# A list scheduler's table of durations is set to other figures

## The chip, the cores and the metric

The kernel runs on one core of one Trainium2 chip. The metric is the device time of one execution in microseconds; the time of a kernel is the median of its runs.

## The reference

One sample of 1024 latent tokens with 1024 channels goes through two layers, in fp32. A prefix of 256 context tokens goes through the first layer's mixer as well. Each layer is a token mixer and then a gated FFN with a convolution, and each of these sub-layers is normalized, modulated by a conditioning vector and added back with a gate.

```python
# layer 0: bidirectional gated linear recurrence (RG-LRU)
ul = seq_conv(hl @ w_x, conv_w, conv_b, CONV_A_PAD)        # latent tokens
uc = seq_conv(hc @ w_x, conv_w, conv_b, CONV_A_PAD)        # context tokens
r = sigmoid(u @ w_r + b_r); i = sigmoid(u @ w_i + b_i)     # blocks of 256 channels, each direction
log_a = 8 * r * log_sigmoid(lam); a = exp(log_a)
h_t = a * h_prev + sqrt(-expm1(2 * log_a)) * (i * u)       # forward and reverse, context first
y = (gelu(hl @ w_gate) * (h_fwd + h_bwd)) @ w_out
# layer 1: short gated convolution
y = (g_b * conv3(g_c * v)) @ w_out
# both layers
y = (silu(conv(g)) * v) @ w_down                           # g, v = h @ w_up, 2816 channels each
```

A modulation is `h * (1 + scale) + shift`; shift, scale and gate are columns of `silu(c) @ ada_w + ada_b`.

## The kernel before

Channels lie on the 128 partitions and tokens along the free axis, so the stream `x` is eight tiles of 128 x 1024. Every fp32 product is three fp32r matmuls over a rounded part and a remainder of both operands (hi·hi, lo·hi, hi·lo). ScalarE writes the rounded part (`wh` of weights, `bh`, `uh`, `hch` of tokens) and VectorE the remainder (`wl`, `bl`, `ul`, `hcl`). The FFN's products are cut into blocks of which seven products replace eight; `s` are its temporaries and its staged weights.

The first layer's mixer goes by the string `ORDER`: `g0` to `g7` are gate products, `x` the products of `w_x` for latent tokens, `ctx` the modulation of the context tokens and their products (`ctx_apply`, L701), `r0` to `r7` the recurrence of 128 channels each (`ri`, L770). `start` (L565) does the norm and the first products; its last part, `shifts`, ends in `softplus` (L522), a row of tiny VectorE operations on 128 x 16 (`sp`) that makes the recurrence's columns. `conv_a` (L710) evicts a product on ScalarE and adds three taps on VectorE (`u<-banks`, `u<-acct`, `u<-uc`; `uc` for context tokens). `ri` evicts into tiles `mx` on ScalarE, multiplies and scans (`TENSOR_TENSOR_SCAN`) on VectorE and puts `x<-x,mx` at its end. A conditioning column is a `dot` on VectorE: a row of weights times `c`, summed (`raw,modc<-raw,ccb`, `acct,mod<-acct,cb`).

All these calls only record operations in a `Plan` (L50 to L178), so that every instruction has line 163. `record` finds what each operation must follow, and ties every matmul to the one before it. `flush` (three times: before the tiles of the recurrence, before the FFN, and at the end) puts them in order. It gives each operation a duration from `cost`, and between engines a delay from `lag`. An operation's `due` time is counted back from the matmuls, which follow each other at their cost. Then, step by step, it takes the engine whose best operation would end first, and issues on it, of those that can start before that end, the one with the earliest `due`:

```python
e = min(best, key=best.get)
i = min((i for i in queue[e] if times(e, i)[0] < best[e]), key=lambda i: (due[i], i))
self.done[i] = free[e] = times(e, i)[1]
```

The engines then run their lists in that order, each waiting for the semaphores that its operations need. The figures of `cost` and `lag` set the order alone; no instruction waits for a modelled time.

Of the kernel before, what the change touches and what calls it, by code (L numbers as in the profile page):

```python
# [8 lines left out]
F32 = mybir.dt.float32  # L9
# [40 lines left out]
class Plan:  # L50
# [48 lines left out]
    @staticmethod  # L99
    def cost(engine, op, a, k):  # L100

        if engine == "sync":
            return 4 * int(np.prod(a[0].shape)) / 360e3
        n = max(int(np.prod(v.shape[1:])) for v in list(a) + list(k.values()) if isinstance(v, bass.AP))
        if engine == "tensor":
            n = a[2].shape[-1]
            return max(n, 128) / 2400 * (4 if a[2].dtype == F32 else 1)
        if engine == "scalar":
            return 0.09 + n * 0.85e-3 + (0.09 if "accum_out" in k else 0)
        if engine == "gpsimd":  # L110
            return 0.15 + n * (2.1e-3 if op == "tensor_tensor" else 0.84e-3)
        return 0.07 + n * (6.25e-3 if op == "reciprocal" else 1.05e-3)

    @staticmethod
    def lag(a, b):

        return 0.0 if a == b else 0.95 if a == "sync" else 1.9 if b == "sync" else 0.2

    def flush(self):
        ops, first, last = self.ops, self.todo, len(self.ops)  # L120
# [1316 lines left out]
```

## Time and profile before

| | us |
|---|---|
| median of 3 runs | 2076.04 |
| lowest and highest run | 2074.9, 2076.44 |
| the profiled execution | 2077.46 |
| its span | 2075.7 |
| TensorE busy | 2035.4 (98%) |
| VectorE busy | 1763.0 (85%) |
| ScalarE busy | 1050.3 (51%) |

The span reaches from the first instruction to the last one of the profiled execution; its time has 1.8 us more around it. TensorE's granted clock is 0.993 of full speed over the span. The busy shares are means over stretches of different kind: the mixer of the first layer takes the first 396 us, the FFNs with the second mixer nearly all of the rest.

### The profile page before, as it was taken

The page shows a single profiled execution, that of the slowest core. Times are in us where ns is not written, and L with a number is a line of the kernel's source. Part 1 is how long each engine was busy: PE and PEld are TensorE (multiplying, and loading weights), DVE is VectorE, ACT ScalarE, POOL GpSimd, SP SyncE. Part 2 cuts the span into 40 slices and gives each one's busy share as a digit, 9 for nine tenths or more (in the row PEclk, how much of TensorE's full clock was granted, in tenths as well). Part 3 has the DMA queues.
Part 4 walks back from the last instruction along what each step waited for, and adds up shares of the span by engine and source line. Part 5 has one row for each costly group of instructions (what it writes and reads, how often), then busy time and mean ns, then how long its engine had stood idle before and what let it go on. Part 6 is the DMA issues. An engine that isn't in the chain of part 4 may idle for free.

```text
span 2075.7 us, 25028 instructions
## 1 busy us (share of the span) xinstructions
PE 2035.4 (98%) x9218; PEld 1682.5 (81%) x9218; DVE 1763.0 (85%) x2624; ACT 1050.3 (51%) x1574; POOL 0.2 (0%) x4
## 2 busy tenths in 40 slices
PE   9899988999999999999999999999999999999998
PEld 7688877787888888878888788888888888878888
DVE  7998999889888898798679988868988887688867
ACT  6456878546544444535255433435544444464345
POOL 0000000000000000000000000000000000000000
PEclk9999999999999999999999999999999999999999
DMA  7464222641344554655361346652233433474345
GB/s 299 155 211 151 72 84 92 208 143 55 119 142 149 170 178 163 181 184 173 92 197 57 122 163 201 224 189 77 88 131 126 143 136 113 136 233 144 111 141 164
DMA packets 103418, 307.05 MB, mean 148 GB/s; under 512 B 10368, under 2 KB 14720, under 8 KB 103168
## 3 DMA queue, kind: packets, MB, share of 16 engines
q1 hardware_dynamic: 103296, 305.46, 44.5%
q8 instruction: 72, 1.18, 0.2%
q14 instruction: 50, 0.41, 0.1%
HBM read 248.80 MB, written 56.62 MB: 147 GB/s over the span
## 4 chain that ended last, share of the span: by engine, by line
PE 82%; DVE 10%; ACT 4%; issue 2%; DMA 1%; SPq 0%; DVEq 0%; ACTq 0%
PE banks L163 82%; DVE mx L163 2%; ACT mx L163 2%; DVE x L163 2%; DVE u L163 1%; DVE wl L163 1%; DVE bl L163 1%; DVE raw L163 1%; DMA s<-bd 1%; ACT bh L163 1%; ACT L163 0%; DVE ul L163 0%; DVE cs L163 0%; DVE acct L163 0%; DMA x<-in_xs 0%
## 5 line engine op out<-in xcount | busy, mean ns | idle before, releaser
L163 PE MATMUL banks<-bl,wh 128*128 128x512 f32 (+1 forms) x2720 | 1050.4, 386 | 6.8 <-DVE bl L163 6.8
L163 PE MATMUL banks<-bh,wh 128*128 128x512 f32 (+1 forms) x2720 | 1053.0, 387 | 3.1 <-ACT wh L163 1.7
L163 PE MATMUL banks<-bh,wl 128*128 128x512 f32 (+1 forms) x2720 | 1050.0, 386 | 1.9 <-DVE wl L163 1.8
L163 PEld LDWEIGHTS banks<-bl,wh 128*128 128x128 f32 x2720 | 511.0, 188 | 117.7 <-DVE bl L163 14.7
L163 PEld LDWEIGHTS banks<-bh,wh 128*128 128x128 f32 x2720 | 511.1, 188 | 108.1 <-ACT wh L163 2.1
L163 PEld LDWEIGHTS banks<-bh,wl 128*128 128x128 f32 x2720 | 511.0, 188 | 108.0 <-DVE wl L163 6.8
L163 ACT ACTIVATE wh<-raw 128x512 fp32r<-128x512 f32 (+2 forms) x386 | 275.6, 717 | 476.3 <-PE banks L163 384.2
L163 DVE TENSOR_TENSOR wl<-raw,wh 128x512 fp32r<-128x512 f32 (+2 forms) x386 | 303.4, 795 | 60.7 <-ACT wh L163 57.3
L163 DVE SCALAR_TENSOR_TENSOR x<-banks,mod,x 128x512 f32<-128x512 f32 (+1 forms) x184 | 132.6, 726 | 90.4 <-PE banks L163 89.6
L163 ACT ACTIVATE s<-banks 128x512 f32<-128x512 f32 x174 | 103.7, 596 | 194.7 <-PE banks L163 191.3
L163 ACT ACTIVATE wh<-s 128x512 fp32r<-128x512 f32 x216 | 135.6, 628 | 110.5 <-DVE s L163 63.6
L163 DVE TENSOR_TENSOR wl<-s,wh 128x512 fp32r<-128x512 f32 x216 | 148.6, 689 | 37.7 <-ACT wh L163 34.1
L163 DVE TENSOR_TENSOR s<-s,banks 128x512 f32<-128x512 f32 x158 | 107.9, 684 | 37.2 <-PE banks L163 36.9
L163 DVE SCALAR_TENSOR_TENSOR x<-s,vec,x 128x504 f32<-128x504 f32 x132 | 96.4, 741 | 10.2 <-ACT x L163 9.0
L163 DVE SCALAR_TENSOR_TENSOR acct<-acct,cb 128x1024 f32<-128x1024 f32 x69 | 84.1, 1219 | 4.4 <-DMA acct<-in_ada 4.4
L163 PE MATMUL banks<-uh,wh 128*128 128x512 f32 (+1 forms) x192 | 70.8, 369 | 8.3 <-ACT mx L163 7.1
L163 PE MATMUL banks<-ul,wh 128*128 128x512 f32 (+1 forms) x192 | 70.4, 367 | 3.1 <-DVE ul L163 3.1
L163 PE MATMUL banks<-uh,wl 128*128 128x512 f32 (+1 forms) x192 | 70.2, 366 | 0.0
L163 ACT ACTIVATE bh<-s 128x512 fp32r<-128x512 f32 x88 | 51.5, 624 | 34.3 <-DMA s<-bd 32.9
L163 ACT ACTIVATE bh<-x,cols 128x512 fp32r<-128x512 f32 x64 | 45.1, 722 | 37.2 <-DVE cols L163 22.1
L163 DVE TENSOR_TENSOR x<-x,s 128x512 f32<-128x512 f32 x90 | 61.0, 686 | 0.8
L163 DVE TENSOR_TENSOR bl<-s,bh 128x512 fp32r<-128x512 f32 x88 | 57.2, 685 | 4.2 <-ACT bh L163 4.1
(152 smaller groups left out, 1708.0 us busy)
## 6 DMA issues: line engine op xcount, KB each, us to landing
raw<-in_wup SPq DMA_DIRECT2D x92, 512.0 KB, 3.5
acct<-in_ada SPq DMA_DIRECT2D x69, 512.0 KB, 3.5
bd<-x SPq DMA_DIRECT2D x48, 512.0 KB, 3.2
s<-bd SPq DMA_DIRECT2D x44, 512.0 KB, 4.4
raw<-in_wdn SPq DMA_DIRECT2D x32, 512.0 KB, 4.2
raw<-in_wdn SPq DMA_DIRECT2D x40, 384.0 KB, 3.4
raw<-in_wbi SPq DMA_DIRECT2D x26, 512.0 KB, 3.9
xd<-x SPq DMA_DIRECT2D x48, 256.0 KB, 2.5
```

The costliest lines, as they stand in the source:

```text
L163: getattr(getattr(self.tc.nc, e), op)(*a, **k)
```

## The change

Only `cost` and `lag` change. A fp32r matmul of n columns is put at (n + 32)/2400 us in place of max(n, 128)/2400. A ScalarE operation costs 0.84 ns a column in place of 0.85, no longer 0.09 us more where it sums, and 0.1 us more for each bias or scale that is a column of its own. On VectorE a scan costs 2.07 ns a column, other operations but the reciprocal 1.04 in place of 1.05, and 0.06 us more for each scalar that is a column. What follows a load on another engine may start 2.0 us after it in place of 0.95. The rows for GpSimd, which has no operation in the plan, are gone.

```diff
--- before.py
+++ after.py
@@ -104,17 +104,17 @@
         n = max(int(np.prod(v.shape[1:])) for v in list(a) + list(k.values()) if isinstance(v, bass.AP))
         if engine == "tensor":
             n = a[2].shape[-1]
-            return max(n, 128) / 2400 * (4 if a[2].dtype == F32 else 1)
+            return max(n, 128) / 2400 * 4 if a[2].dtype == F32 else (n + 32) / 2400
         if engine == "scalar":
-            return 0.09 + n * 0.85e-3 + (0.09 if "accum_out" in k else 0)
-        if engine == "gpsimd":
-            return 0.15 + n * (2.1e-3 if op == "tensor_tensor" else 0.84e-3)
-        return 0.07 + n * (6.25e-3 if op == "reciprocal" else 1.05e-3)
+            columns = sum(0.1 for name in ("bias", "scale") if isinstance(k.get(name), bass.AP))
+            return 0.09 + n * 0.84e-3 + columns
+        columns = sum(0.06 for name in ("scalar", "scalar1") if isinstance(k.get(name), bass.AP))
+        return 0.07 + n * {"reciprocal": 6.25e-3, "tensor_tensor_scan": 2.07e-3}.get(op, 1.04e-3) + columns
 
     @staticmethod
     def lag(a, b):
 
-        return 0.0 if a == b else 0.95 if a == "sync" else 1.9 if b == "sync" else 0.2
+        return 0.0 if a == b else 2.0 if a == "sync" else 1.9 if b == "sync" else 0.2
 
     def flush(self):
         ops, first, last = self.ops, self.todo, len(self.ops)
```

TensorE's list is the same before and after. The lists of the other engines differ in the order alone. Three places on VectorE follow.

The first place is VectorE around the modulation of the context tokens. `sp` is softplus, `u<-uc` and `u<-acct` are conv taps of the products behind `shifts`, `raw,modc<-raw,ccb` a dot for the context's columns `cols`, and `cs_104`, `hcl` the context tokens before and after the split. Before:

```order
L163 SCALAR_TENSOR_TENSOR u<-acct,vec,u 128x1022
L163 SCALAR_TENSOR_TENSOR u<-uc,vec,u 128x1022
L163 SCALAR_TENSOR_TENSOR raw,modc<-raw,ccb 128x1024 x2
L163 TENSOR_TENSOR cols<-modc,vec 128x8
L163 TENSOR_TENSOR cols<-cols,vec 128x8
L163 SCALAR_TENSOR_TENSOR cs_104<-xc,cols,cs_104 128x256
L163 TENSOR_TENSOR cols<-modc,vec 128x8
L163 SCALAR_TENSOR_TENSOR cs_104<-xc,cols,cs_104 128x256
L163 TENSOR_TENSOR wl<-raw,wh 128x1024
L163 SCALAR_TENSOR_TENSOR cs_104<-xc,cols,cs_104 128x256 x2
L163 SCALAR_TENSOR_TENSOR hcl<-cs_104,cols,hch 128x256 x2
```

and in the change, where two taps, a `wl`, two dots and ten operations of softplus stand just ahead of this piece:

```order
L163 TENSOR_SCALAR sp<-sp 128x16
L163 TENSOR_TENSOR sp<-sp 128x16
L163 TENSOR_SCALAR sp<-vec 128x16
L163 SCALAR_TENSOR_TENSOR sp<-sp 128x16
L163 SCALAR_TENSOR_TENSOR u<-acct,vec,u 128x1023
L163 SCALAR_TENSOR_TENSOR u<-uc,vec,u 128x1023
L163 SCALAR_TENSOR_TENSOR raw,modc<-raw,ccb 128x1024 x2
L163 TENSOR_TENSOR cols<-modc,vec 128x8
L163 TENSOR_TENSOR cols<-cols,vec 128x8
L163 SCALAR_TENSOR_TENSOR cs_104<-xc,cols,cs_104 128x256
L163 TENSOR_TENSOR cols<-modc,vec 128x8
L163 SCALAR_TENSOR_TENSOR cs_104<-xc,cols,cs_104 128x256 x2
```

The rest of softplus, two more taps and a `wl` have moved ahead of the last dots, and so of `cols`, `cs_104` and `hcl`.

The second place is VectorE between the recurrences of two channel tiles (`uc` and `u` are the two inputs of a recurrence, `mx` its tiles). Before:

```order
L163 SCALAR_TENSOR_TENSOR mx<-mx,uc 128x256
L163 SCALAR_TENSOR_TENSOR mx<-mx,u 128x1024
L163 TENSOR_TENSOR mx<-mx 128x1024
L163 TENSOR_TENSOR x<-x,mx 128x1024
L163 SCALAR_TENSOR_TENSOR acct,mod<-acct,cb 128x1024
L163 SCALAR_TENSOR_TENSOR mx<-mx,u 128x1024
```

and now:

```order
L163 SCALAR_TENSOR_TENSOR mx<-mx,uc 128x256
L163 SCALAR_TENSOR_TENSOR acct,mod<-acct,cb 128x1024
L163 SCALAR_TENSOR_TENSOR mx<-mx,u 128x1024
L163 TENSOR_TENSOR mx<-mx 128x1024
L163 TENSOR_TENSOR x<-x,mx 128x1024
L163 SCALAR_TENSOR_TENSOR mx<-mx,u 128x1024
```

The dot `acct,mod<-acct,cb`, which stood behind `x<-x,mx`, has moved ahead of the scan of `u` whose result goes into that `x`. A few rows further down come the `u<-banks` taps of a `w_x` product. Before:

```order
L163 SCALAR_TENSOR_TENSOR u<-mx,u 128x1024
L163 TENSOR_TENSOR mx<-mx 128x1280
L163 TENSOR_TENSOR u<-u,mx 128x1024
L163 SCALAR_TENSOR_TENSOR u<-banks,vec,u 128x1023
L163 SCALAR_TENSOR_TENSOR u<-banks,vec,u 128x1022
L163 SCALAR_TENSOR_TENSOR u<-banks,vec,u 128x1023
L163 TENSOR_TENSOR wl<-raw,wh 128x1024
L163 SCALAR_TENSOR_TENSOR uc<-mx,uc 128x256
```

and now:

```order
L163 SCALAR_TENSOR_TENSOR u<-mx,u 128x1024
L163 SCALAR_TENSOR_TENSOR uc<-mx,uc 128x256 x2
L163 SCALAR_TENSOR_TENSOR u<-banks,vec,u 128x1023
L163 SCALAR_TENSOR_TENSOR u<-banks,vec,u 128x1022
L163 SCALAR_TENSOR_TENSOR u<-banks,vec,u 128x1023
L163 SCALAR_TENSOR_TENSOR acct,mod<-acct,cb 128x1024
L163 TENSOR_TENSOR mx<-mx 128x1280
L163 TENSOR_TENSOR u<-u,mx 128x1024
```

The taps have moved ahead of `mx<-mx` and `u<-u,mx`, and a `uc<-mx,uc` has come ahead of the taps.

The third place is VectorE at the last two recurrences, where the first operands of the `w_out` product are split (`bl_87`). Before:

```order
L163 TENSOR_TENSOR u<-u,mx 128x1024
L163 TENSOR_TENSOR wl<-raw,wh 128x1024
L163 SCALAR_TENSOR_TENSOR uc<-mx,uc 128x256
L163 TENSOR_TENSOR uc<-uc,mx 128x256
L163 SCALAR_TENSOR_TENSOR mx<-mx,uc 128x256
L163 SCALAR_TENSOR_TENSOR mx<-mx,u 128x1024
L163 TENSOR_TENSOR bl_87<-x,bh_86 128x512
L163 TENSOR_TENSOR wl<-raw,wh 128x1024
L163 TENSOR_TENSOR bl_87<-x,bh_86 128x512 x6
```

and now:

```order
L163 TENSOR_TENSOR bl_87<-x,bh_86 128x512
L163 TENSOR_TENSOR wl<-raw,wh 128x1024
L163 TENSOR_TENSOR bl_87<-x,bh_86 128x512 x2
L163 SCALAR_TENSOR_TENSOR u<-mx,u 128x1024
L163 TENSOR_TENSOR bl_87<-x,bh_86 128x512
L163 TENSOR_TENSOR wl<-raw,wh 128x1024
L163 SCALAR_TENSOR_TENSOR uc<-mx,uc 128x256
L163 TENSOR_TENSOR u<-u,mx 128x1024
L163 TENSOR_TENSOR uc<-uc,mx 128x256
L163 SCALAR_TENSOR_TENSOR mx<-mx,uc 128x256
L163 TENSOR_TENSOR bl_87<-x,bh_86 128x512
L163 SCALAR_TENSOR_TENSOR mx<-mx,u 128x1024
```

Of the `wl<-raw,wh` rows the second of each piece is the same instruction. Five rows of the scan chain stand behind it now, and `bl_87` rows ahead of it.

## Rows read from the trace of the kernel before

**Rows 1.** The busy time of each engine, its share of the span and its instructions
```profile
PE 2035.4 (98%) x9218; PEld 1682.5 (81%) x9218; DVE 1763.0 (85%) x2624; ACT 1050.3 (51%) x1574; POOL 0.2 (0%) x4
```

**Rows 2.** Busy time by stretch (length, then PE, PEld, DVE, ACT, POOL, granted clock, DMA)
```profile
126.00:142.00 16.00, 14.04 (x67) 11.14 (x65) 15.76 (x36) 8.29 (x13) 0.00 (x0) 1.00 0.61 197
142.00:160.00 18.00, 18.00 (x137) 18.00 (x138) 16.69 (x35) 8.17 (x10) 0.00 (x0) 0.91 0.58 178
...
208.00:253.00 45.00, 45.00 (x217) 37.91 (x216) 44.50 (x46) 36.92 (x38) 0.00 (x0) 1.00 0.25 82
...
899.00:2068.00 1169.00, 1166.58 (x5284) 967.02 (x5284) 956.58 (x1455) 539.25 (x873) 0.00 (x0) 1.00 0.44 143
```

**Rows 3.** TensorE's waits, 103 to 396 us: total, times, longest (us)
```profile
PE banks L163 <- ACT mx L163: 7.1, 2, 4.8
PE banks L163 <- DVE ul L163: 3.1, 1, 3.1
...
PE banks L163 <- DVE hcl L163: 1.8, 4, 0.9
```

**Rows 4.** The chain of waits in order of time: start, length, what
```profile
141.96 47.25 PE banks L163 x293
...
1148.00 710.65 PE banks L163 x3135
```

**Rows 5.** Timeline of VectorE, 94 to 103 us: start, length, operation, [idle before <-releaser]
```profile
96.32 2.60 DVE L163 SCALAR_TENSOR_TENSOR u<-banks,vec,u 128x1023 f32<-128x1023 f32 x2 [0.94 <-ACT u L163]
98.83 1.22 DVE L163 SCALAR_TENSOR_TENSOR raw<-raw,ccb 128x1024 f32<-128x1024 f32 x1
```

**Rows 6.** Timeline of VectorE, 142 to 161 us
```profile
143.35 0.17 DVE L163 TENSOR_SCALAR sp<-sp 128x16 f32<-128x16 f32 x1
...
144.50 1.22 DVE L163 TENSOR_TENSOR wl<-raw,wh 128x1024 fp32r<-128x1024 f32 x1
...
150.44 0.17 DVE L163 TENSOR_SCALAR sp<-sp 128x16 f32<-128x16 f32 x1
...
151.87 1.28 DVE L163 SCALAR_TENSOR_TENSOR u<-acct,vec,u 128x1023 f32<-128x1023 f32 x1
...
159.07 1.27 DVE L163 SCALAR_TENSOR_TENSOR u<-uc,vec,u 128x1023 f32<-128x1023 f32 x1
```

**Rows 7.** Timeline of TensorE near 142 and 889 us
```profile
141.96 0.38 PE L163 MATMUL banks<-hcl,wh 128*128 128x256 f32 x1 [0.91 <-DVE hcl L163]
...
889.29 0.50 PE L163 MATMUL banks<-bh,wh 128*128 128x512 f32 x1 [1.67 <-ACT wh L163]
```

**Rows 8.** Timeline of VectorE, 250 to 372 us
```profile
250.78 1.48 DVE L163 TENSOR_TENSOR mx<-mx 128x1280 f32<-128x1280 f32 x1
...
253.31 3.91 DVE L163 SCALAR_TENSOR_TENSOR u<-banks,vec,u 128x1023 f32<-128x1023 f32 x3
...
352.93 1.20 DVE L163 TENSOR_TENSOR u<-u,mx 128x1024 f32<-128x1024 f32 x1
...
356.82 2.35 DVE L163 TENSOR_TENSOR_SCAN mx<-mx,u 128x1024 f32<-128x1024 f32 x1
...
359.91 1.23 DVE L163 TENSOR_TENSOR wl<-raw,wh 128x1024 fp32r<-128x1024 f32 x1 [0.15 <-ACT wh L163]
...
371.85 0.69 DVE L163 TENSOR_TENSOR bl<-x,bh 128x512 fp32r<-128x512 f32 x1 [0.91 <-ACT bh L163]
```

**Rows 9.** Timeline of ScalarE, 243 to 896 us
```profile
243.18 4.16 ACT L163 ACTIVATE mx<-mx,sp 128x1280 f32<-128x1280 f32 x3 [1.06 <-DVE x L163]
...
251.00 1.19 ACT L163 ACTIVATE u<-banks,vec 128x1024 f32<-128x1024 f32 x1
...
358.81 1.06 ACT L163 ACTIVATE wh<-raw 128x1024 fp32r<-128x1024 f32 x1 [2.75 <-PE banks L163]
...
887.57 1.15 ACT L163 ACTIVATE bh<-s 128x512 fp32r<-128x512 f32 x2 [2.68 <-DMA s<-bd]
...
895.56 1.15 ACT L163 ACTIVATE bh<-s 128x512 fp32r<-128x512 f32 x2 [1.30 <-DMA s<-bd]
```

## The prediction

> **What bounds the kernel now.** I read the busy times first, then a table of stretches, then what TensorE waited for, then the chain of waits, and last single places on VectorE, ScalarE and TensorE. The reader should see in the first that TensorE (PE) is busy 98% of the span, so that only 2075.7 − 2035.4 = 40.3 us of it are idle [rows 1]. The diff leaves TensorE's own list of instructions as it is: the planner ties every matmul to the one before. So the time changes only by making those 40 us larger or smaller. The table of stretches shows where the others are the limit [rows 2]. From 126 to 142 us VectorE (DVE) is busy 15.76 of 16 us: it works without a pause on the shift of the normalized stream, the column sums for the conditioning (the `dots`) and the context tokens. From 208 to 253 us it is busy 44.50 of 45. From 899 to 2068 us TensorE has only 2.4 us of idle in 1169. The FFN is therefore TensorE's, and the first 400 us belong to VectorE nearly as much. TensorE's waits between 103 and 396 us confirm it: 7.1 us on ScalarE's (ACT) `mx`, 3.1 on VectorE's `ul`, 1.8 in four waits on VectorE's `hcl` [rows 3]. The chain shows what a delay there is worth. Behind the last `hcl` wait stand 47.25 us of TensorE work without a gap, and the FFN has 710.65 us in one piece [rows 4]. So lateness at 142 us cannot be made up until 189 us, and what is late at 396 us stays late to the end.
>
> **The change part by part.** No instruction is added or taken out; 1417 of 2512 VectorE instructions, 465 of 1544 on ScalarE and 178 of 648 loads and stores stand elsewhere in their engine's list, most by one or two places. I walked the new lists with the durations of the trace. Places where nothing late results I cost at nothing; their cover is TensorE's list, which is contiguous there.
>
> 1. At 95 us VectorE waits 0.94 us for ScalarE before three conv steps [rows 5]. Two dots move ahead of these steps and fill the wait. A dot takes 1.22 us, so VectorE gains the wait once, and the first conv step is late by 2 x 1.22 − 0.94 = 1.5 us, with slack behind it. Worth between 0 and −0.94; I take −0.5.
>
> 2. From 127 to 160 us lies the main cost. Before, VectorE does two conv steps, four context dots and then at once the chain `cols`, `cs`, `hcl` of the context tokens, for which TensorE waits. The 14 remaining tiny softplus steps come later, in two groups, 144.50 − 143.35 = 1.15 us and 151.87 − 150.44 = 1.43 us long, and two more conv steps later still, 1.28 and 1.27 us [rows 6]. Now all of these stand ahead of the last context dots. That is 1.15 + 1.43 + 1.28 + 1.27 = 5.1 us more VectorE work before the first `hcl`, on an engine with no idle time to take it. TensorE already waits for `hcl`, the last time 0.91 us [rows 7], so its lateness passes on whole: **+5.1**. It then goes into the 47.25 us piece [rows 4]; the work that left 143 to 160 us gives nothing back, because TensorE has 18.00 of 18 us there [rows 2]. Lower bound: only softplus counts, if the conv steps find idle time, 2.6. Upper bound: TensorE's granted clock, 0.91 in 142 to 160 us [rows 2], falls as much once more behind the longer wait, 18 x 0.09 = 1.6, so 6.7. I take 5.1, as both rows show VectorE full.
>
> 3. At 243 us a dot (1.22 us as in [rows 5]) moves ahead of the scan that ends in `x<-x,mx`; ScalarE's three `mx` activations already wait 1.06 us for that `x` [rows 9]. They come that much later. Behind them ScalarE now evicts the conv bank (`u<-banks`) before the second of two square roots, about as long as a dot, so it delivers `u` at the same 251.00 + 1.19 = 252.2 us as before. But VectorE comes to its conv steps 2.1 us sooner: two multiplies, 253.31 − 250.78 = 2.53 us, went behind them [rows 8], and a step on 256 columns, which I put at 0.4 us, came ahead. It waits for `u` from 251.2 to 252.2: **+1.0** of idle on a saturated engine. Lower bound 0, if idle time further on absorbs it; upper 1.2, the dot.
>
> 4. At 359 us `wl<-raw,wh` needs ScalarE's `wh`, which itself waits 2.75 us for TensorE, and VectorE waits only 0.15 us for it [rows 8, 9]. In the new list less VectorE work stands ahead of that `wl`. Five steps of the scan chain went behind it, the first at 352.93 us and the last to 359.17 us, 6.24 us less one other `wl` of 1.22, so 5.0 us; four `bl` of 0.69 us came ahead, 2.8 [rows 8]. VectorE stands until `wh` comes, 5.0 − 2.8 = 2.2 us. It gets back the 0.91 us that it waited at 371.85 us [rows 8]: **+1.3**, since the scan chain behind decides when the mixer ends. Bounds 0 (TensorE frees `wh` sooner) and 2.2.
>
> 5. In the FFN's second part, at 889.29 us, TensorE waits 1.67 us for a `wh` [rows 7]. That `wh` now stands ahead of two `bh` which wait 2.68 us for a load, so the wait goes [rows 9]. But two other `bh` slip behind a pair that starts only at 895.56 us after its own load [rows 9], some 3 us later than they ran, and by the slack of TensorE there I expect a new wait of about 2 us. Net **+0.3**, bounds −1.7 and +1.7. Everywhere else in the FFN the moved pieces are a few tenths long and run ahead of use.
>
> Sum: −0.5 + 5.1 + 1.0 + 1.3 + 0.3 = +7.2 us. The profiled execution took 2077.46 us, so it would take 2084.7; it lies 1.4 above the median of the runs, 2076.04, which becomes **2083.2 us**. Lower ends together: −0.94 + 2.6 + 0 + 0 − 1.7 = 0, 2076.0; upper ends: 0 + 6.7 + 1.2 + 2.2 + 1.7 = 11.8, 2087.8.
>
> **The rivals.** *No change.* All that moves is covered: TensorE's 98% is the same list, and whatever idle time VectorE has between 160 and 396 us takes up what is late. For it: [rows 1], and the long pieces in [rows 4]. Against it: the wait on `hcl` is a wait of TensorE itself, and nothing before 189 us can absorb it. It would leave the 5.1 us at 142 us, give back most of it before 396 us, and end within 2076 to 2080.
>
> *Faster.* The new table prices scans at twice the old figure and column operands separately, so that the VectorE and ScalarE steps of the scans may come in an order which is right where the old one was not. The place is 253 to 352 us: TensorE waits there 7.1 us on `mx` and 3.1 on `ul` [rows 3]. If those waits vanish, −10.2, and the push of part 2 stays, +4.6 with part 1, the time is 2076.0 − 5.6 = 2070.4. It decides from the point at which more than 4.6 of the 10.2 us go. For it: ul's matmuls come from work which the new list puts about 1 us earlier. Against it: the chain into these waits goes through VectorE, which is full before them, and its work to be done by then is the same. More than the 40 us of idle can't be had: in the piece of 710.65 us 3135 matmuls follow each other every 710.65 / 3135 = 0.227 us with nothing to wait for [rows 4], and no order of the other engines shortens that. The Trainium skill (Perfetto Trace Analysis, Identifying the Most-Contended Engine) holds the busy share of matmuls a poor measure of the room left on TensorE and points, among others, to the busy share of weight loads. By that share, 81% here [rows 1], some 19% of 2076, 394 us, would be room for a better order; the long piece says that it is not, and the rule gets no chance of its own.
>
> *Slower still.* The FFN's seams miss their loads: part 5 comes to its upper end, 1.4 us more than I take, and parts 2 and 4 as well, 1.6 and 0.9 more. It gives 2083.2 + 3.9 = 2087.1 and is inside the range.
>
> **How the numbers follow.** About 0.2% (4.15 us) is what a measurement of this kernel tells from no change, so `same` is 2071.9 to 2080.2. My forecast with its upper cases has 0.60; it needs part 2 whole and no more than half of it given back. No change has 0.27: the walk through the lists is long, and each slack in it was read from one execution. Faster has 0.13: a walk with fixed durations shows new waits more readily than vanished ones. The range leaves out the outer half of the faster case and a little above the upper ends: 2072 to 2088.5. The slower case's own range is 2080.2 to 2088.5.
>
> **What would show it.** Right: in the changed kernel TensorE waits about 5 us in all for the first `hcl` near 140 to 147 us, and its long piece starts near 147 us instead of 142. VectorE waits about 1 us for ScalarE's `u` near 258 us, and over 2 us for a `wh` near 365 us; the long piece of TensorE work that opens the FFN starts some 7 us late, and the FFN is as long as before. Wrong: the long piece starts at 142 to 143 us, in which case part 2 had slack that I didn't see; or it starts late, and TensorE's waits on `mx` and `ul` shrink by as much; or the FFN itself changes by over 2 us.

## The result, and the profile after

The changed kernel takes 2086.73 us (median of 4 runs, 2084.51 to 2088.53), the kernel before 2075.89 (4 runs, 2074.9 to 2076.44). The ratio is 1.0051 with an interval of 1.0039 to 1.0063: 10.6 us slower, between 8.1 and 13.1. Run once more (e11 below) it gave 1.0049 (1.0036 to 1.0061). The forecast was +7.2 us: the direction is right, the size lies just under the interval.

The page of the changed kernel's profile (an execution of 2084.51 us, the shortest of its four) answers to [rows 1]:

```profile
span 2082.7 us, 25041 instructions
...
PE 2037.4 (98%) x9218; PEld 1685.3 (81%) x9218; DVE 1765.1 (85%) x2624; ACT 1055.5 (51%) x1574; POOL 0.2 (0%) x4
```

The same matmuls, and 45.3 us without one where there were 40.3. The busy shares would let nobody find the loss. The chain of waits does, beside [rows 4] (start, length, what):

```profile
148.04 46.14 PE banks L163 x290
...
403.15 63.38 PE banks L163 x282
...
1153.90 699.94 PE banks L163 x3088
```

The long piece that began at 141.96 us begins at 148.04, but three matmuls further on in the list; the same matmul is 5.6 us late. The FFN's first piece, at 396.14 us before, begins at 403.15, 7.0 late, and its longest, at 1148.00 before, 5.9 late. So in these two executions the loss is made before 400 us and the FFN adds nothing to it. Nor is it one lateness kept. TensorE's matmuls come in the same order in both kernels, so they can be compared one by one: the changed kernel's are 5.0 us late at 189 us, 3.7 at 260 and 7.0 at 396 (times of the kernel before). A part of what the first 150 us lose is taken up, and the recurrences lose 3.3 us anew behind 260 us. Of TensorE's waits from 103 to 406 us (total, times, longest) [rows 3] are the counterpart:

```profile
PE banks L163 <- ACT mx L163: 10.8, 2, 6.2
PE banks L163 <- DVE ul L163: 3.6, 3, 2.1
PE banks L163 <- DVE u L163: 3.0, 1, 3.0
PE banks L163 <- DVE bl L163: 2.5, 1, 2.5
PE banks L163 <- DVE hcl L163: 2.0, 2, 1.8
```

The first `hcl` in VectorE's timeline of the kernel before (start, length, operation, idle before and its releaser):

```profile
136.33 0.87 DVE L163 SCALAR_TENSOR_TENSOR hcl<-cs,cols,hch 128x256 fp32r<-128x256 f32 x2
```

and in the changed kernel the places that steps 1 to 4 of the prediction name:

```profile
95.24 0.62 DVE L163 SCALAR_TENSOR_TENSOR cs<-u,cols,cs 128x384 f32<-128x384 f32 x1 [1.20 <-DMA u<-in_w]
...
130.31 0.17 DVE L163 TENSOR_SCALAR sp<-sp 128x16 f32<-128x16 f32 x1
...
134.01 1.28 DVE L163 SCALAR_TENSOR_TENSOR u<-acct,vec,u 128x1023 f32<-128x1023 f32 x1
135.20 1.28 DVE L163 SCALAR_TENSOR_TENSOR u<-uc,vec,u 128x1023 f32<-128x1023 f32 x1
...
142.01 0.87 DVE L163 SCALAR_TENSOR_TENSOR hcl<-cs,cols,hch 128x256 fp32r<-128x256 f32 x2
...
256.98 3.92 DVE L163 SCALAR_TENSOR_TENSOR u<-banks,vec,u 128x1023 f32<-128x1023 f32 x3 [0.89 <-ACT u L163]
...
365.03 1.22 DVE L163 TENSOR_TENSOR wl<-raw,wh 128x1024 fp32r<-128x1024 f32 x1 [1.70 <-ACT wh L163]
```

The last steps of softplus and two taps stand between 130.31 and 136.4 us, and the first `hcl` comes after them, at 142.01 instead of 136.33 us, 5.7 late. The waits forecast at 1.0 us for `u` and 2.2 us for a `wh` are there with 0.89 and 1.70 us. TensorE, at the first place and at the seam in the FFN:

```profile
142.54 0.39 PE L163 MATMUL banks<-hcl,wh 128*128 128x256 f32 x1 [1.79 <-DVE hcl L163]
...
901.77 0.50 PE L163 MATMUL banks<-bh,wh 128*128 128x512 f32 x1 [1.49 <-ACT bh L163]
```

The wait for `hcl` is only 1.79 us although `hcl` is 5.7 late. TensorE had become late before: its granted clock was at the lower level, 0.50, from 103 to 107 us (length, then busy time of PE, PEld, DVE, ACT, POOL, granted clock, DMA), in the changed kernel

```profile
103.00:107.00 4.00, 3.94 (x12) 3.43 (x13) 3.90 (x6) 2.88 (x7) 0.00 (x0) 0.50 0.48 151
```

and at full speed in the kernel before:

```profile
103.00:107.00 4.00, 4.00 (x21) 3.31 (x21) 3.90 (x8) 3.57 (x7) 0.00 (x0) 1.00 0.81 243
```

Those 4 us had 12 matmuls instead of 21, and that cost nothing that can be seen, since `hcl` came later still: in the second profile of the changed kernel (e11) the granted clock of the same 4 us was 0.76, and the long piece begins at 148.00 us all the same. There TensorE waits 1.15 us for a `wl` near 129 us, as it does not in the first profile, and again 1.79 for the first `hcl`. At the seam, the wait of 1.67 us at 889.29 us [rows 7] is gone and one of 1.49 us has come for the `bh` that slipped, as step 5 had it.

### The profile page after: what moved, and what is told of

It reads as the page before. It is cut to its first block, busy times and chain, and to the rows that moved or that the text cites. A ratio compares the mean times of both kernels' runs of the same rounds, so it can differ in the third digit from the quotient of the medians.

```text
span 2082.7 us, 25041 instructions
## 1 busy us (share of the span) xinstructions
PE 2037.4 (98%) x9218; PEld 1685.3 (81%) x9218; DVE 1765.1 (85%) x2624; ACT 1055.5 (51%) x1574; POOL 0.2 (0%) x4
## 4 chain that ended last, share of the span: by engine, by line
PE 79%; DVE 15%; ACT 3%; issue 2%; DMA 1%; SPq 0%; DVEq 0%; ACTq 0%
PE banks L163 79%; DVE mx L163 3%; DVE x L163 3%; DVE u L163 2%; DVE bl L163 2%; DVE wl L163 2%; ACT mx L163 1%; DVE acct L163 1%; DVE raw L163 1%; DVE ul L163 1%; DVE s L163 1%; DMA s<-bd 1%; ACT L163 0%; DVE cs L163 0%; DMA x<-in_xs 0%
## 5 line engine op out<-in xcount | busy, mean ns | idle before, releaser
L163 PE MATMUL banks<-uh,wh 128*128 128x512 f32 (+1 forms) x192 | 69.6, 362 | 10.8 <-ACT mx L163 10.8
L163 DVE TENSOR_TENSOR x<-x 128x512 f32<-128x512 f32 x88 | 60.4, 687 | 1.1
```

The lines of the kernel that those rows point to most:

```text
L163: getattr(getattr(self.tc.nc, e), op)(*a, **k)
```

## The experiments

`flush` runs three times: up to about 170 us (norm, shifts, context), to about 400 us (recurrences), and from the first FFN on. The experiments work out the orders of both tables in full, each with its own clocks, and issue one of them in each of the three parts. All zeros gives the order before, all ones that of the change.

```diff
+    PICK = (1, 0, 0)
     def flush(self):
+        plans = [self.plan(t) for t in (0, 1)]
+        out = plans[self.PICK[self.turn]]
+        for i in out:
+            engine, op, a, k = self.ops[i][:4]
+            getattr(getattr(self.tc.nc, engine), op)(*a, **k)
+        self.turn += 1
```

Microseconds below are the ratio less one, times 2076; in brackets its interval.

**One part at a time** (`PICK` is (1, 0, 0), (0, 1, 0), (0, 0, 1)).

> The new table orders only the first part of the program (up to about 170 us: norm, shifts, softplus, context products), the old one the recurrences and the FFNs. Theory A (the softplus steps and two conv taps ahead of the context chain are the main cost): TensorE's long piece starts 4 to 6 us later than in the kernel before, and the time is 4 to 6 us longer. Theory B (what is late there is taken up in the recurrences, and the changed recurrences or FFN make the loss): the long piece is late as well, but the time is within 2 us of the kernel before.

> The new table orders only the recurrences (about 170 to 400 us). Theory A: +1 to +2.5 us (the dot ahead of a scan, and the wait for a wh near 359 us). Theory B (the recurrences make the loss): +5 us or more. A third one, that the new prices of scans and columns help here and are hidden by the late start: -1 to -3 us.

> The new table orders only the part from the first FFN on (about 400 us to the end). Theory A: within 1 us of the kernel before, since the one profile of the changed kernel has its FFN 0.3 us shorter. Theory C (the four runs of the changed kernel scatter over 4 us where those before scatter over 1.5, so the FFN's order makes it late in most executions): +2 to +4 us, with a like scatter.

The first part alone: +5.2 us [+3.1 to +7.3]; TensorE's long piece begins at 147.53 us. The recurrences alone: +3.1 [+1.2 to +5.0]. The FFNs alone: +2.3 [+0.4 to +4.2]. The three make 10.6, the change's own figure; each is known to some 2 us, and within that the parts add. By its time, theory B (within 2 us) falls for the first part. The chain of its profile shows less than its time does:

```profile
147.53 45.36 PE banks L163 x290
...
398.98 85.15 PE banks L163 x378
...
1863.91 204.15 PE banks L163 x1038
```

Matmul for matmul that is 5.1 us late at the long piece (it too begins three matmuls further on), and 2.8 at the start of the FFN and 2.0 behind its last seam, which are at 396.14 and 1861.92 us before. So in this pair of executions nearly half of the first part's lateness is taken up before the FFN, 1.4 us of it by the end of the long piece. There the kernel before loses time of its own: both have a granted clock of 0.76 from 142 to 149 us, but in the kernel before that spell lies behind the last wait for `hcl`, and in e1 ahead of it. The traces also make the gap smaller than it is by the medians: the profile of the kernel before is 1.4 us longer than its median, that of e1 1.1 shorter.

In the second run's profile TensorE is 0.5 us early at 189 us and 3.2 late at 396. Its waits for `mx` are 10.7 us, as in the change, where the first run has the 7.1 of the kernel before. VectorE's timeline of that run shows both waits of steps 3 and 4, with the first part as it was:

```profile
251.55 3.92 DVE L163 SCALAR_TENSOR_TENSOR u<-banks,vec,u 128x1023 f32<-128x1023 f32 x3 [0.88 <-ACT u L163]
...
361.21 1.23 DVE L163 TENSOR_TENSOR wl<-raw,wh 128x1024 fp32r<-128x1024 f32 x1 [2.30 <-ACT wh L163]
```

The FFN, which theory A put within 1 us, loses 2.3: that is theory C's range, though its runs scatter over 4.7 us and those before over 4.0, and the interval reaches down into theory A's 1 us.

**Softplus and two taps moved back**, behind the last `hcl`, all else as in the change:

```diff
+        if self.turn == 0:
...
+            for i in reversed(back):
+                out.remove(i)
+                out.insert(min([j for j, s in enumerate(out) if i in self.ops[s][5]] + [len(out)]), i)
```

Here `back` names the 14 softplus steps and the two taps. In e4 they are put directly behind the last `hcl`, in e7 (with the last two steps of softplus) each as late as its first user allows, as the diff has it.

> The changed kernel with 14 softplus steps and two conv taps moved back on VectorE, behind the last hcl; all else as in the changed kernel. Theory A: 5 to 6 us less than the changed kernel, so about 2080.5 and the long piece at 142 to 143 us. Theory B: the gain is lost again in the recurrences, within 2 us of the changed kernel's 2086.7.

> As e4, but the moved softplus steps and the two taps stand as late as their users allow: behind the context taps (uc), not ahead of them. In e4 a new wait of 2.4 us came at 150.7 us, where the moved 5.1 us stood ahead of the uc taps that free TensorE's banks. Theory A (the 5 us of VectorE work are the loss of part 1, and e4 only moved them in front of the next user): 4 to 5 us less than the changed kernel, about 2082, and the long piece without that wait. Rival (the recurrences are late whatever part 1 does): as e4, 2085.6.

e4 gives +9.8 us [+7.3 to +12.5] against the kernel before, hardly less than the change. Its TensorE shows why:

```profile
150.74 0.39 PE L163 MATMUL banks<-hch,wl 128*128 128x256 f32 x1 [2.60 <-DVE wl L163]
```

The work now stands ahead of the next `wl`, which TensorE needs as much, and its last wait has become 2.60 us. (Not the context taps, as I had it when I wrote down what to expect of e7.) e7 takes it out of that way too: +6.4 [+4.2 to +8.7], 4.2 us less than the change. In its profile TensorE's long piece has no wait in it and begins at

```profile
143.01 45.36 PE banks L163 x290
```

So the 5 us of VectorE work are the loss of the first part, and what counts is every consumer behind it on VectorE. The first part's changes on ScalarE and in the loads are still in e7, and its 6.4 us are, within the noise, the 5.4 that the other two parts make alone. e7's runs lie between 2079.46 and 2085.63 us, its profile is of the shortest; why it scatters is open.

**Which figure does it.** All three parts go by the second order, whose table is changed. e5 has the old durations and the new delay behind a load; e6 the new durations and the old delay. Durations are pairs, the old and the new one; of e5 one pair stands here, and the others go the same way:

```diff
# e5
-            return old, max(n, 128) / 2400 * 4 if a[2].dtype == F32 else (n + 32) / 2400
+            return old, old
# e6
-    LAG = (0.95, 2.0)
+    LAG = (0.95, 0.95)
```

> Of the new table only the delay behind a load (2.0 for 0.95) is taken; every duration is the old one. In this order 21 softplus steps and 8 conv taps stand ahead of the first hcl on VectorE, as in the changed kernel (21 and 9). Theory A (the delay alone is what pushes softplus and taps ahead of the context chain): +3.5 to +5 us at TensorE's long piece and about as much at the end, 2080 to 2081. Rival (it takes the durations as well): within 2 us of the kernel before.

> Of the new table all but the delay behind a load is taken. In this order 16 softplus steps and 7 conv taps stand ahead of the first hcl (7 and 7 in the kernel before), so 0.17 to 0.2 us for each of 9 tiny steps, about 1.7 us. Theory A: +1.5 to +2.5 us at the long piece, and with what e2 and e3 showed for the later parts +5 to +7 at the end if those come from the durations, +2 if they come from the delay. Rival (the delay is the whole loss): within 1.5 us of the kernel before.

The delay alone: +9.3 us [+6.6 to +11.8], almost the whole loss and twice theory A's figure. All but the delay: −1.0 [−2.9 to +1.0], no difference. But e6 isn't harmless in each place. TensorE waits there for the context chain as in the change:

```profile
141.91 0.39 PE L163 MATMUL banks<-hcl,wh 128*128 128x256 f32 x1 [1.17 <-DVE hcl L163]
```

In its chain the long piece, the start of the FFN and the piece behind the last seam are these,

```profile
147.40 45.35 PE banks L163 x290
...
400.97 63.38 PE banks L163 x282
...
1861.51 204.37 PE banks L163 x1038
```

and in the kernel before the last two are:

```profile
396.14 85.15 PE banks L163 x378
...
1861.92 204.15 PE banks L163 x1038
```

Matmul for matmul e6 is 5.0 us late at 147 us, 4.8 at 401, and 0.4 early behind the last seam. From the first FFN to the last seam e6 takes 1460.5 us, the kernel before 1465.8. So durations and delay each push softplus ahead of the context chain, and in the FFN they work against each other. That made the next two runs.

**The FFNs alone, with the durations and with the delay.** The tables are those of e6 (for e9) and e5 (for e10), issued in the last part alone:

```diff
-    PICK = (1, 1, 1)
+    PICK = (0, 0, 1)
```

> The old table for the first 400 us; from the first FFN on the new durations, but the old delay of 0.95 behind a load. In e6 TensorE was 4.6 us late at 390 us and 0.2 us early at the end, so its FFN was 4.8 us shorter than the profiled one of the kernel before. Theory D (the durations mend the FFN's seams, and the delay spoils them): 2 to 5 us less than the kernel before, 2071.5 to 2074.5, and TensorE's waits at 889 us and behind are gone. Rival (the FFN of e6 was short because it began late and its loads had had more time): within 1.5 us of the kernel before.

> The old table for the first 400 us; from the first FFN on the old durations with the new delay of 2.0 us behind a load. Theory D: 2.5 to 5 us more than the kernel before (e5 was 2.6 us later at its end than at 352 us in its profile). Rival (the late FFN of e5 comes from its late start): within 1.5 us of the kernel before.

e9: 2071.73 us, −3.7 us [−5.6 to −1.9], so it beats both kernels. e10: +3.7 [+1.9 to +5.6]. By the times theory D holds. The seam at 890 us in e9 and in e10:

```profile
891.46 0.49 PE L163 MATMUL banks<-bh,wh 128*128 128x512 f32 x1 [0.62 <-ACT bh L163]
```

```profile
896.53 0.56 PE L163 MATMUL banks<-bh,wh 128*128 128x512 f32 x1 [3.08 <-ACT bh L163]
```

At these seams ScalarE's `bh` waits for loads of `s` from `bd`, so the queue's own timeline tells more (start, time to issue, transfer). In the kernel before

```profile
859.48 0.32 SPq L163 DMA_DIRECT2D s<-bd  x1
...
872.77 3.04 SPq L163 DMA_DIRECT2D s<-bd  x2
...
879.11 2.68 SPq L163 DMA_DIRECT2D s<-bd  x2
...
884.79 0.32 SPq L163 DMA_DIRECT2D s<-bd  x1
885.16 0.43 SPq L163 DMA_DIRECT2D ad<-x  x1
...
889.55 1.52 SPq L163 DMA_DIRECT2D s<-bd  x2
```

and in e9

```profile
864.84 8.76 SPq L163 DMA_DIRECT2D s<-bd  x3
...
876.28 9.33 SPq L163 DMA_DIRECT2D s<-bd  x5
...
889.90 0.43 SPq L163 DMA_DIRECT2D ad<-x  x1
```

By 886 us the kernel before has issued six loads of `s` and a store, e9 eight loads, and the store only after them. That the earlier loads are what ends the wait is read from these rows; no run moved a load alone. Compared matmul by matmul with the kernel before, from 396 us on, e9 gains 4.2 us, 2.0 of them between 887 and 910 us, at this seam, and e10 loses 2.6, 1.9 of them here. Single traces must be read with care at this seam, since executions with the same order differ there: the traces of e1 and e2, whose FFN order is that of the kernel before, are 1.0 and 1.7 us faster here than its own trace. But e6 and e5, which have the FFN orders of e9 and e10, bear them out, with 2.8 us gained and 1.5 lost.

**Only the matmul's price**, in the FFNs alone: as e10, with the old delay, and the pair of e5's diff above left as it was.

> As e9, but of the new durations only the matmul's: (n + 32)/2400 us, 0.2267 us for 512 columns, which is the spacing of the 3135 matmuls in the trace of the kernel before (710.65/3135 = 0.2267), where the old price is 0.2133. Theory D1 (the old price makes the FFN's due times 6% too early, 100 us over an FFN of 1670 us, so that what TensorE needs soon is ranked behind what it needs late): the whole of e9's gain, 2071 to 2072.5. Theory D2 (the column operands' price makes it): within 1.5 us of the kernel before.

−1.7 us [−3.5 to +0.4]: the interval holds most of theory D2's range and only just reaches D1's. The full gain of e9 is not shown to come from this price; which of the durations adds the rest is open.

**The error turned round**: on the kernel before, five softplus steps and a tap moved from ahead of the context dots to behind the last `hcl`, with the code of e7 and other names in `back`.

> The kernel before, with its old table, with five softplus steps and one conv tap (2.2 us of VectorE work) moved from ahead of the last context dots to behind the last hcl: the change's own error turned round. Theory A: TensorE's 1.8 us of waits for hcl go, the long piece starts 1.5 to 1.8 us earlier, and 1 to 1.5 us of it are left at the end, about 2074.8. Rival (something else sets that time, ScalarE's hch or a wl): no change.

+0.6 us [−1.2 to +2.5]: nothing gained. There is no trace of one of the executions that were compared, so whether TensorE's waits for `hcl` went and came back elsewhere is open. Theory A isn't borne out here; that moving work off the front of the context chain pays was shown only from the change's side (e7).

**The change again.**

> The changed kernel again, in the order of the change, to see a second profile and more runs: its first profile was 7.05 us longer than that of the kernel before, its median 10.8. If the FFN's loads decide the difference, this profile shows it behind 880 us, with the lateness up to 400 us as in the first (about 7 us); if it lies in the mixer, the lateness at 400 us differs.

2085.94 us, ratio as above. Its profile shows TensorE 6.5 us late at 396 us and 6.1 at its last matmul, the first profile 7.0 and 6.7. Neither profile shows a loss in the FFN. But the first is the shortest execution of its set (2084.51 of a median of 2086.73), the second within 0.1 us of it, and the profile of before is 1.4 us longer than its median, so the two traces understate the difference by about 3.6 us. The seam near 890 us is one place: e3 and e4 have the change's FFN order too, and lose 1.1 us there against the kernel before, where the two profiles of the change gain 0.7 and 0.8. Whether it is the only one, no trace shows.

## Why the prediction came out as it did

**What bounds the kernel: right but for one sentence.** TensorE's list and its 98% stayed, and the time moved mostly with its idle time: of the 7.0 us by which the span grew, 5.0 are idle time and 2.0 matmuls that took longer (2037.4 for 2035.4 us busy). That one, that lateness at 142 us can't be made up until 189 us, was too strong: 5.6 us have become 5.0 there in the change, and 5.1 have become 3.7 in e1. The 47.25 us of [rows 4] hold the spell at the lower clock that the prediction read in [rows 2]. Its upper bound had that spell cost as much once more; in e1 it came ahead of the wait and cost less.

**Steps 1 and 2, +4.6 forecast, +5.2 [+3.1 to +7.3] measured (e1): right in place and cause, and in size by the time.** Step 1's gain of 0.5 did not come: the wait for `u` is gone, but VectorE now waits before it for a load (1.20 us in the change, 0.63 in e1). The first `hcl` is 5.7 us late where step 2 had 5.1. That the step was the 5 us of VectorE work, and not its place alone, is shown by e4 and e7 together. The sign that I had named, 5 us of waiting for `hcl`, did not come: TensorE's waits for it are 2.0 us in all, before 1.8. The rest went to the lower clock at 103 to 107 us, or, where the clock fell less, to a `wl` near 129 us (1.02 us in e1, 1.15 in e11), and to ScalarE's `hch` (0.35). How much of the 5.7 us is left at 396 us is less sure: e1's profile says 2.8 us, the change's profile against e2's 3.8, and by e1's time 5.2 are left at the end.

**Steps 3 and 4, +2.3 forecast, +3.1 [+1.2 to +5.0] measured (e2): right.** Waits of 0.88 and 2.30 us stand where 1.0 and 2.2 were worked out. In the change the second is 1.70 us: VectorE comes to it 4.4 us later than in e2, the `wh` only 3.8 later.

**Step 5, +0.3 forecast, +2.3 [+0.4 to +4.2] measured (e3): the mis-sized term.** The step saw the right seam and the right two moves: the wait for `wh` went, and one for `bh` came (1.49 us in the change, 2.05 in e3, for "about 2"). It then put everything else in the FFN at nothing, because the moved pieces are short and run ahead of use. e9 and e10 show that the FFN's order is worth 3.7 us in either direction. One sign of being wrong was an FFN that changes by over 2 us; by the time of e3 it does, by the traces it doesn't. The seam's loads of `s` were counted by what waited on ScalarE, not by how the list of loads had moved.

**The rivals.** *No change* needed most of the 5.1 us to be taken up before 396 us. In e1's profile about half is, but its time and the change's are past the 2080 us that this rival allowed, and the recurrences, where it wanted the lateness taken up, lose in their new order by themselves (e2). *Faster* wanted the waits on `mx` and `ul` to vanish; `mx` grew from 7.1 to 10.8 us. But a gain from the new durations was there, in the FFN, where I had seen none: e9. *Slower still*, at 2087.1 us, comes nearest to the measured 2086.73, but not by its sum: it took steps 2, 4 and 5 at their upper ends, and of the three only step 5's is seen (e3). So that number is partly luck. Mine was 3.4 us short: the three parts miss by 0.6, 0.8 and 2.0 us, the first two within their intervals, the third just outside.

**What none of the steps asked**: which figure moves the order. I priced the moves and not the table. The delay alone makes nearly all of the loss (e5), the durations none in sum (e6). Per load the new delay is the truer one: the kernel before shows

```profile
acct<-in_ada SPq DMA_DIRECT2D x69, 512.0 KB, 3.5
```

(transfers, size, median us from issue to landing), and the planner's cost of 1.46 us for 512 KB makes 3.5 with a delay of 2.0, and 2.4 with 0.95. My reading is that a later landing leaves idle time on VectorE in the plan, into which the planner puts work that is not due, though the real VectorE has none (15.76 of 16 us busy [rows 2]). That reading is argued; no run shows the plan's inside.

## What to carry to other kernels

A table of durations that is truer to each instruction can give a worse order, so try its figures one by one and part by part: here one of them lost 9.3 us, and the others, kept to the FFN, won 3.7. When an engine is full, work moved ahead of a chain makes the chain late by its whole duration, and moved behind that chain it delays the next consumer; it is free only behind the last one that TensorE waits for. Look at the list of loads at a seam as closely as at the engines that wait for them.

## What the runs showed of the chip that I had not expected

TensorE's granted clock fell to 0.50 from 103 to 107 us behind a wait of 3.04 us in the changed kernel, and in e9 as well (0.50 in the same stretch, behind 2.66 us), while the kernel before had 1.00 behind a wait of 2.65 us; e9 is the fastest of all kernels here nevertheless. Up to 400 us e9 has the order of the kernel before. From 142 to 149 us it is the other way round: e9 has 1.00, the kernel before 0.76. There the spell costs something, since no wait for another engine comes behind it before 189 us. The same 293 matmuls that take 47.25 us before [rows 4] take 45.80 in e9:

```profile
143.11 45.80 PE banks L163 x293
```

e2 has the spell where e9 has it, e3 and e10 where the kernel before has it. So one order can meet it in either place, and what decides between them no run shows. In the change a lower clock ahead of a wait for another engine cost nothing that can be seen; e9's long piece begins 1.15 us later than that of the kernel before, and whether the early spell made it late is open.
